# Starts of the SBUF buffers in a two-layer hybrid attention encoder: from multiples of 128 bytes to multiples of 512

## The chip, the cores and the metric

The kernel runs on one core of a Trainium2 chip. The metric is the device time of one execution in microseconds (us); of several executions the median is given. The engines are called PE (TensorE, its weight loads shown apart as PEld), DVE (VectorE), ACT (ScalarE), POOL (GpSimd) and SP (SyncE, which issues most of the DMAs).

## The reference, cut to what matters

Two layers over a sequence of 512 tokens of width 1024, all in float32. Each layer normalises its input, projects it with one wide matrix, runs three attention branches side by side, and merges them through sigmoid gates.

```python
for l in range(DEPTH):                                  # DEPTH = 2
    mod = c_act @ w_ada[l] + b_ada[l]
    shift, scale, gate = [m[:, None, :] for m in split_cols(mod, (D, D, D))]
    h = rms_norm(x, g_pre[l]) * (1.0 + scale) + shift
    (cq, ckv, kr, za, qb_, kb_, vb_, zb, qc, kc, vc, zc, gcols) = split_cols(h @ w_in[l], IN_SPLITS)
    o_a = (mla_branch(cq, ckv, kr, ...) * jax.nn.silu(za)) @ w_o_mla[l]
    o_b = (swa_branch(qb_, kb_, vb_, sink[l], swa_bias) * jax.nn.silu(zb)) @ w_o_swa[l]
    o_c = (diff_branch(qc, kc, vc, ...) * jax.nn.silu(zc)) @ w_o_diff[l]
    g = jax.nn.sigmoid(gcols).reshape(B, S, N_BRANCH, D)
    y = (g[:, :, 0] * o_a + g[:, :, 1] * o_b + g[:, :, 2] * o_c) @ w_out[l]
    x = x + gate * rms_norm(y, g_post[l])
```

The branches are multi-head latent attention (MLA, 8 heads), sliding-window attention with sinks (SWA, 8 heads over 2 key heads), and differential attention (4 heads of two score maps each).

## The kernel before, in words

Precision comes from splitting: a float32 operand is written as a high part in the type float32r and a low part that holds the rest, and a product of two split operands is three matmuls, high by high, high by low and low by high (mm3, lines 87 to 90). The normed and transposed input of a layer lies in hTh and hTl for the whole layer. wunit (lines 103 to 117) loads 512 KB of weights into a tile wr, from which ACT writes the high part (wh, line 82) and DVE the low part (wl, line 85); proj_T (lines 464 to 470) then runs 8 x 3 matmuls of 128x128 by 512 columns, with a piece of wh or wl as the stationary operand and a piece of hTh or hTl as the moving one. In pe.matmul(o, a, b) the first input, a, is the stationary operand and b the moving one; the profile names the moving one first (ps_dn<-hTh,wh).

- merge_steps (lines 528 to 571) multiplies the outputs of a branch, split into pairs of tiles u, by the branch's output weights: moving u, stationary wh or wl.
- prep, within mla_attention, makes a head's queries and keys from latents (cl, in tiles big) with weights in the tile x5: moving big, stationary x5.
- The scores take both operands from tiles op; the products with the values take the transposed probabilities (pt) as the moving operand and the values (tiles big) as the stationary one. Transposes on PE (line 704) have ident as the moving operand.
- out_phase (lines 1017 to 1066) multiplies by w_out in two halves of 512 columns, 8 x 4 x 3 matmuls each. Here the weights move, and the stationary operands are the merged tiles in op and pt. In the second half the first two of four weight tiles lie in tiles big (wunit with big true, lines 105 and 106), the other two in wh and wl, so that for each of four row tiles twelve matmuls read big and the next twelve wh and wl.
- At the start, layer0_input (lines 338 to 371) computes three of the gate inputs with weights split into tiles pt: moving hTh or hTl, stationary pt.

The order of the instructions on each engine is set when the program is built, by a scheduler of the framework that goes by a simulated timeline; priorities are given in the code. Tiles are taken by T (lines 64 to 67). A tag has a fixed number of buffers (line 62), and the buffers of a tag get their place, in each partition, when the tag is first used, one after another. A buffer takes its bytes per partition rounded up to 32. The first tile of the program, ident, begins at byte 16,512, which is 128 past a multiple of 512. ident, ones and onesr take 512 bytes each, then mhalf 96 and epsc 32, so that the eight buffers big begin at 18,176, 256 past a multiple of 512; the rest follows in this way. Some small tiles are 32 columns wide although fewer are used (LINE, line 23, in lines 151, 168, 177 and 398), which makes 128 bytes of each and keeps every large buffer on a multiple of 128. Where the buffers begin, in bytes past a multiple of 512, the same for all buffers of a tag, since their sizes are multiples of 512:

| buffers | before |
|---|---|
| ident, ones, onesr, rq, rk | 128 |
| big, hTh, hTl, o, op, wr, p, u, pt, zz | 256 |
| wh, wl, tf, ta, x5, kp | 384 |

Within a tile the matmuls read from offsets that are multiples of 512 bytes, so these numbers hold for their operands too (the matmuls of one column, and two that read the small tile rb, apart).

Of the kernel before, what the change touches and what calls it, by code (L numbers as in the profile page):

```python
# [17 lines left out]
P = 128  # L18
S = 512
D = 1024  # L20
KT = D // P
NT = S // P
LINE = 32
DEPTH = 2
EPS = 1e-6
NEG = -1e30
# [25 lines left out]
def hybrid_kernel(ctx, tc, x, c, w_ada, b_ada, g_pre, g_post, w_in, g_q, w_uq, g_kv, w_ukv,  # L52
# [6 lines left out]
    pe, act, dve, pool, sp = nc.tensor, nc.scalar, nc.vector, nc.gpsimd, nc.sync  # L59
# [4 lines left out]
    def T(tag, shape, dt=F32, bufs=None):  # L64
        count[0] += 1
        return sb.tile(shape, dt, tag=tag, name=f"{tag}_{count[0]}",
                       bufs=bufs or BUFS.get(tag, 1))

    def stat(n):
        return T("st", [P, n], F32, 24)  # L70
# [3 lines left out]
    def Q(tag):  # L74
        count[0] += 1
        return ps.tile([P, S], F32, tag=tag, name=f"ps_{tag}_{count[0]}", bufs=PB[tag])
# [41 lines left out]

    WOFF = [100]

    ident = T("ident", [P, P])
    make_identity(nc, ident)
    ones = T("ones", [P, P])
    dve.memset(ones, 1.0)
    onesr = T("onesr", [P, P], F32R)
    dve.tensor_copy(out=onesr, in_=ones)
    mhalf = T("mhalf", [P, 24])
    dve.memset(mhalf, -0.5)
    epsc = T("epsc", [P, 1])
    dve.memset(epsc, EPS)  # L130

    x1d = dr.tile([S, D], F32, tag="x1d", name="x1d")
# [15 lines left out]
        return res  # L148

    xt0 = [T("big", [P, D]) for _ in range(NT)]  # L150
    cT = T("cT", [P, LINE])[:, 0:KT]
    sp.dma_start(out=cT, in_=c.rearrange("b (p k) -> p (b k)", k=KT))
    src0 = mod_load(0, 0, 1, ("wh", "wl"))
    prm = [T("tf", [P, P]) for _ in range(2)]
# [2 lines left out]
    for k, src, n in ((PR_GQ, g_q, 2), (PR_GKV, g_kv, 1), (PR_GSUB, g_sub, 1)):  # L157
        pool.dma_start(out=prm[1][k - 32:k - 32 + n * DEPTH, :],
                       in_=src.rearrange("l (a b) -> (l a) b", b=P))
# [3 lines left out]
    prT = []  # L163

    for i, n in enumerate((32, PR_ROWS - 32)):
        prps = Q("tr")
        pe.transpose(prps[:, 0:n], prm[i][0:n, :], ident[0:n, 0:n])
        prT.append(T(f"prT{i}", [P, LINE])[:, 0:n])
        dve.tensor_copy(out=prT[i], in_=prps[:, 0:n])

    def par(l, k, i=0, n=1):
        lo = k + l * PR_STEP[k] + i
        return prT[lo // 32][:, lo % 32:lo % 32 + n]

    th = stat(KT)
    act.activation(out=th, in_=cT, func=AF.Tanh, scale=0.5)
    cact = T("cact", [P, LINE])[:, 0:KT]
    dve.scalar_tensor_tensor(out=cact, in0=th, scalar=1.0, in1=cT, op0=ALU.add, op1=ALU.mult)
    dve.tensor_scalar(out=cact, in0=cact, scalar1=0.5, scalar2=None, op0=ALU.mult)

    amul = [T(f"amul{l}", [P, KT]) for l in range(DEPTH)]
    ashf = [T(f"ashf{l}", [P, KT]) for l in range(DEPTH)]

    stts, amuls, sums = [], [], []

# [209 lines left out]

    rq = T("rq", [P, S])
    rk = T("rk", [P, NT, 64])
    sinkt = T("sinkt", [P, LINE])[:, 0:DEPTH * 8]
    lam_neg = []
    gsub = []  # L400
    bias_s = []
# [2 lines left out]
    def setup_small():  # L404
        sp.dma_start(out=rk, in_=rope_k.rearrange("(t p) c -> p t c", p=P))
        sp.dma_start(out=rq, in_=rope_q)
        sp.dma_start(out=sinkt, in_=sink.rearrange("(o l) h -> o (l h)", o=1).broadcast_to([P, DEPTH * 8]))
        for l in range(DEPTH):
            li = 0.8 - 0.6 * math.exp(-0.3 * l)
            lt = T("tf", [P, 4, 64])  # L410
            for i, src in enumerate((lam_q1, lam_k1, lam_q2, lam_k2)):
                sp.dma_start(out=lt[:, i], in_=src[l:l + 1, :].broadcast_to([P, 64]))
            e = stat(2)
            for i in range(2):
                dve.tensor_tensor(out=lt[:, 2 * i], in0=lt[:, 2 * i], in1=lt[:, 2 * i + 1],
                                  op=ALU.mult)
                dve.tensor_reduce(out=e[:, i:i + 1], in_=lt[:, 2 * i], axis=AX.X, op=ALU.add)
            act.activation(out=e, in_=e, func=AF.Exp)
            nl = T(f"nl{l}", [P, 1])
            dve.tensor_scalar(out=nl, in0=e[:, 1:2], scalar1=e[:, 0:1], scalar2=-li,  # L420
                              op0=ALU.subtract, op1=ALU.add)
            lam_neg.append(nl)
            gs = T(f"gs{l}", [P, 1])
            dve.tensor_scalar(out=gs, in0=par(l, PR_GSUB), scalar1=0.5 * (1.0 - li), scalar2=None,
                              op0=ALU.mult)
            gsub.append(gs)
# [721 lines left out]
    with behind(loads[-1]):  # L1148
        setup_small()
# [70 lines left out]
```

## Time and profile before

| what | value |
|---|---|
| median of 3 runs | 1195.54 us (1195.54 to 1196.23) |
| the profiled execution | 1194.84 us |
| its span, first to last instruction | 1192.9 us |
| mean granted TensorE clock | 0.992 |
| matmul records | 5428 |
| DMA | 146.86 MB, 123 GB/s on the mean |

A row of the timeline gives the start and the length of an instruction, its engine and line, what it writes and reads, and the shapes. The length of a matmul is modelled to the end of its way through the array, while the next one starts before that; so the distance between starts is read from the first numbers of two rows, and the length from the second. In a row of groups stand the count, the busy time, the mean length in ns and the idle time before it. A row of windows gives, for a stretch of the span, its length, the busy time and the instructions of PE, PEld, DVE, ACT and POOL, the granted clock, the share of the DMA engines and GB/s.

### The profile page before, as it was taken

The page shows a single profiled execution, that of the slowest core. Times are in us where ns is not written, and L with a number is a line of the kernel's source. Part 1 is how long each engine was busy: PE and PEld are TensorE (multiplying, and loading weights), DVE is VectorE, ACT ScalarE, POOL GpSimd, SP SyncE. Part 2 cuts the span into 40 slices and gives each one's busy share as a digit, 9 for nine tenths or more (in the row PEclk, how much of TensorE's full clock was granted, in tenths as well). Part 3 has the DMA queues.
Part 4 walks back from the last instruction along what each step waited for, and adds up shares of the span by engine and source line. Part 5 has one row for each costly group of instructions (what it writes and reads, how often), then busy time and mean ns, then how long its engine had stood idle before and what let it go on. Part 6 is the DMA issues. An engine that isn't in the chain of part 4 may idle for free.

```text
span 1192.9 us, 15536 instructions
## 1 busy us (share of the span) xinstructions
PE 1163.9 (98%) x5428; PEld 949.2 (80%) x5428; DVE 845.5 (71%) x1754; ACT 632.3 (53%) x1250; POOL 182.5 (15%) x226
## 2 busy tenths in 40 slices
PE   5899999999999999999999999999999999999997
PEld 4778788878887888888888888888888888888886
DVE  7956676998865687866577557688785468776554
ACT  5454464655543457654357446565555345665432
POOL 4310212111210010102111011122121001010120
PEclk8899999999999999999999999999999999999999
DMA  9637532255355333443454433224433433334442
GB/s 328 200 89 215 179 110 71 75 157 168 104 155 159 98 85 81 114 118 112 149 176 136 109 104 87 72 67 121 140 102 84 107 85 90 87 101 111 133 161 86
DMA packets 169522, 146.86 MB, mean 123 GB/s; under 512 B 7679, under 2 KB 146999, under 8 KB 169444
## 3 DMA queue, kind: packets, MB, share of 16 engines
q1 hardware_dynamic: 166148, 140.08, 40.8%
q10 hardware_dynamic: 3168, 5.77, 1.4%
q8 instruction: 43, 0.70, 0.2%
q14 instruction: 35, 0.29, 0.1%
q0 software_dynamic: 128, 0.01, 0.0%
HBM read 135.83 MB, written 14.20 MB: 126 GB/s over the span
## 4 chain that ended last, share of the span: by engine, by line
PE 85%; DVE 6%; DMA 4%; issue 3%; POOL 1%; ACT 1%; SPq 1%; DVEq 0%; POOLq 0%; ACTq 0%
PE ps_dn L88 20%; PE ps_dn L90 20%; PE ps_dn L89 20%; PE ps_tr L704 5%; PE ps_sc L90 2%; PE ps_sc L88 2%; PE ps_sc L89 2%; PE ps_av L713 1%; PE ps_av L714 1%; DMA wr<-in_w_ada 1%; PE ps_sc L953 1%; PE ps_sc L952 1%; DVE o L205 1%; DMA wr<-in_w_in 1%; PE ps_pj L88 1%
## 5 line engine op out<-in xcount | busy, mean ns | idle before, releaser
L88 PE MATMUL ps_dn<-hTh,wh 128*128 128x512 f32 x840 | 335.8, 400 | 0.4 <-DVE zz L479 0.3
L90 PE MATMUL ps_dn<-hTh,wl 128*128 128x512 f32 x840 | 334.2, 398 | 0.3 <-DVE wl L85 0.3
L89 PE MATMUL ps_dn<-hTl,wh 128*128 128x512 f32 x840 | 333.9, 398 | 0.0
L85 DVE TENSOR_TENSOR wl<-wr,wh 128x1024 fp32r<-128x1024 f32 x141 | 178.9, 1269 | 105.2 <-ACT wh L82 104.3
L82 ACT ACTIVATE wh<-wr 128x1024 fp32r<-128x1024 f32 x141 | 149.1, 1058 | 174.2 <-PE ps_dn L89 119.0
L90 PEld LDWEIGHTS ps_dn<-hTh,wl 128*128 128x128 f32 x840 | 158.3, 188 | 36.5 <-DVE wl L85 0.7
L88 PEld LDWEIGHTS ps_dn<-hTh,wh 128*128 128x128 f32 x840 | 158.6, 189 | 35.5 <-DVE zz L479 0.6
L89 PEld LDWEIGHTS ps_dn<-hTl,wh 128*128 128x128 f32 x840 | 158.6, 189 | 35.1
L82 ACT ACTIVATE pt<-ps_tr 128x512 fp32r<-128x512 f32 x136 | 79.0, 596 | 69.0 <-PE ps_tr L704 67.8
L85 DVE TENSOR_TENSOR pt<-ps_tr,pt 128x512 fp32r<-128x512 f32 x136 | 92.3, 686 | 32.3 <-ACT pt L82 31.4
L775 POOL TENSOR_SCALAR p<-p,st 128x512 f32<-128x512 f32 x64 | 52.2, 835 | 283.9 <-DVE st L773 246.8
L704 PE MATMUL ps_tr<-ident,p 128*128 128x128 f32 x544 | 92.3, 273 | 0.5 <-POOL p L775 0.3
L704 PEld LDWEIGHTS ps_tr<-ident,p 128*128 128x128 f32 x544 | 69.6, 141 | 19.7 <-POOL p L775 1.2
L90 PE MATMUL ps_dn<-u,wl 128*128 128x512 f32 x192 | 76.6, 399 | 0.0
L88 PE MATMUL ps_dn<-u,wh 128*128 128x512 f32 x192 | 76.6, 399 | 0.0
L89 PE MATMUL ps_dn<-u,wh 128*128 128x512 f32 x192 | 76.0, 396 | 0.0
L963 POOL TENSOR_SCALAR ta<-ta,st 128x512 f32<-128x512 f32 x32 | 26.8, 837 | 312.6 <-DVE st L962 132.0
L894 POOL TENSOR_SCALAR p<-p,st 128x256 f32<-128x256 f32 (+1 forms) x64 | 41.4, 666 | 160.2 <-DVE st L892 126.2
L770 DVE TENSOR_REDUCE st<-ps_sc 128x1 f32<-128x512 f32 x64 | 43.5, 687 | 22.0 <-PE ps_sc L90 21.5
L771 ACT ACTIVATE p<-ps_sc,st 128x512 f32<-128x512 f32 x64 | 43.8, 686 | 28.0 <-DVE st L770 27.5
L886 ACT ACTIVATE p<-p,st 128x256 f32<-128x256 f32 (+1 forms) x64 | 35.6, 557 | 20.6 <-DVE st L884 20.4
L959 ACT ACTIVATE p<-p,st 128x512 f32<-128x512 f32 x32 | 23.1, 723 | 38.1 <-DVE st L957 38.0
(345 smaller groups left out, 2109.6 us busy)
## 6 DMA issues: line engine op xcount, KB each, us to landing
wr<-in_w_in SPq DMA_DIRECT2D x105, 512.0 KB, 3.8
wr<-in_w_ada SPq DMA_DIRECT2D x32, 512.0 KB, 3.6
wr<-in_w_out SPq DMA_DIRECT2D x16, 512.0 KB, 3.7
big<-in_w_ada SPq DMA_DIRECT2D x10, 512.0 KB, 7.8
big<-in_x SPq DMA_DIRECT2D x8, 512.0 KB, 5.3
wr<-in_w_o_mla SPq DMA_DIRECT2D x8, 512.0 KB, 3.5
wr<-in_w_o_swa SPq DMA_DIRECT2D x8, 512.0 KB, 3.5
wr<-in_w_o_diff SPq DMA_DIRECT2D x8, 512.0 KB, 3.6
```

The costliest lines, as they stand in the source:

```text
L82: return act.activation(out=out_, in_=in_, func=AF.Copy, scale=scale)
L85: return (eng or dve).tensor_tensor(out=out_, in0=a, in1=b, op=ALU.subtract)
L88: pe.matmul(o, ah, bh, start=start, stop=False)
L89: pe.matmul(o, ah, bl, start=False, stop=False)
L90: pe.matmul(o, al, bh, start=False, stop=stop)
L704: pe.transpose(tr[:, i * P:(i + 1) * P], b, ident)
L770: dve.tensor_reduce(out=nm[:, t:t + 1], in_=s, axis=AX.X, op=ALU.max, negate=True)
L771: act.activation(out=pr[:, t], in_=s, func=AF.Exp, bias=nm[:, t:t + 1], accum_out=sm[:, t:t + 1])
L775: pool.tensor_scalar(out=pr[:, t], in0=pr[:, t], scalar1=rr[:, t:t + 1], scalar2=1.0, op0=ALU.mult, op1=ALU.mult)
L886: act.activation(out=pr[:, i, :w], in_=pr[:, i, :w], func=AF.Exp, bias=nm[:, i:i + 1], accum_out=sm[:, i:i + 1])
L894: pool.tensor_scalar(out=pr[:, i, :w], in0=pr[:, i, :w], scalar1=rr[:, i:i + 1], scalar2=1.0, op0=ALU.mult, op1=ALU.mult)
L963: pool.tensor_scalar(out=pc[1], in0=pc[1], scalar1=rr[:, 1:2], scalar2=1.0, op0=ALU.mult, op1=ALU.mult)
```

## The change

The small tiles that live through the whole program are taken first, before ident: mhalf (now 8 columns), epsc, cT, cact, amul and ashf for both layers, lamc (new, 4 columns, which takes the place of nl0, nl1, gs0 and gs1) and sinkt (24 columns). Together they take 384 bytes, so that ident begins at 16,896, a multiple of 512. LINE is gone.

```diff
-LINE = 32
...
+    mhalf = T("mhalf", [P, 8])
+    epsc = T("epsc", [P, 1])
+    cT = T("cT", [P, KT])
+    cact = T("cact", [P, KT])
+    amul = [T(f"amul{l}", [P, KT]) for l in range(DEPTH)]
+    ashf = [T(f"ashf{l}", [P, KT]) for l in range(DEPTH)]
+    lamc = T("lamc", [P, 2 * DEPTH])
+    sinkt = T("sinkt", [P, 24])
     ident = T("ident", [P, P])
...
-    mhalf = T("mhalf", [P, 24])
     dve.memset(mhalf, -0.5)
-    epsc = T("epsc", [P, 1])
     dve.memset(epsc, EPS)
...
-    cT = T("cT", [P, LINE])[:, 0:KT]
...
-        prT.append(T(f"prT{i}", [P, LINE])[:, 0:n])
+        prT.append(T(f"prT{i}", [P, 32])[:, 0:n])
...
-    cact = T("cact", [P, LINE])[:, 0:KT]
...
-    amul = [T(f"amul{l}", [P, KT]) for l in range(DEPTH)]
-    ashf = [T(f"ashf{l}", [P, KT]) for l in range(DEPTH)]
...
-    sinkt = T("sinkt", [P, LINE])[:, 0:DEPTH * 8]
...
-            nl = T(f"nl{l}", [P, 1])
+            nl = lamc[:, 2 * l:2 * l + 1]
...
-            gs = T(f"gs{l}", [P, 1])
+            gs = lamc[:, 2 * l + 1:2 * l + 2]
```

As built, every buffer of 512 bytes or more a partition that TensorE reads (ident, ones, onesr, big, hTh, hTl, op, wh, wl, u, p, pt, tf, ta, x5), and wr, o, zz, rq, rk and kp besides, begins at a multiple of 512 bytes. The instructions of every engine stand in the same order in both programs, with the same waits, and nothing else in them differs but the addresses, the width of the memset of mhalf, and the names lamc for nl and gs.

More of the change, by code (lines that the diff above doesn't have):

```diff
@@ L406, in setup_small @@
         sp.dma_start(out=rq, in_=rope_q)
-        sp.dma_start(out=sinkt, in_=sink.rearrange("(o l) h -> o (l h)", o=1).broadcast_to([P, DEPTH * 8]))
+        sp.dma_start(out=sinkt[:, 0:DEPTH * 8], in_=sink.rearrange("(o l) h -> o (l h)", o=1).broadcast_to([P, DEPTH * 8]))
         for l in range(DEPTH):
```

## The prediction

> **What bounds the kernel now.** I read the page first, then the windows, then TensorE's timeline. The page gives the span and the busy times, and the chain that ended last.
>
> ```profile
> span 1192.9 us, 15536 instructions
> PE 1163.9 (98%) x5428; PEld 949.2 (80%) x5428; DVE 845.5 (71%) x1754; ACT 632.3 (53%) x1250; POOL 182.5 (15%) x226
> PE 85%; DVE 6%; DMA 4%; issue 3%; POOL 1%; ACT 1%; SPq 1%; DVEq 0%; POOLq 0%; ACTq 0%
> ```
>
> PE is busy 98% of the span and 85% of the last chain runs on it; DVE, the next engine, is at 71%. The windows say where PE is the whole story:
>
> ```profile
> 0.00:60.00 60.00, 40.39 (x187) 35.60 (x188) 48.84 (x122) 28.48 (x55) 24.77 (x29) 0.89 0.79 262
> 60.00:130.00 70.00, 69.11 (x304) 54.37 (x303) 44.48 (x115) 35.95 (x94) 4.81 (x6) 1.00 0.57 162
> 130.00:260.00 130.00, 127.68 (x618) 102.38 (x617) 101.65 (x173) 75.70 (x156) 26.94 (x33) 0.99 0.38 110
> 260.00:600.00 340.00, 339.92 (x1580) 277.10 (x1579) 245.37 (x521) 178.81 (x323) 44.66 (x56) 1.00 0.43 123
> 640.00:1165.00 525.00, 525.00 (x2448) 426.71 (x2447) 363.83 (x740) 284.07 (x552) 73.95 (x91) 1.00 0.37 106
> ```
>
> The first engine column is PE. From 130 us on it idles for 2.3 us in the first window and 0.1 us in the 865 us of the last two. So the time after 130 us is the number of matmuls times the distance from one start to the next, which I call a slot. A matmul's 0.39 us reaches into the next slot, so a wait shorter than some 0.16 us does not show as idle time. Only two things can shorten this program without taking matmuls away: shorter slots, or fewer such hidden waits.
>
> **What the change does to each engine.** Every engine's instructions stand in the same order in both programs, with the same waits; only addresses differ, and one memset (128x24 becomes 128x8). So the question is what a start address does to a slot. The trace of before answers a part of it, because its buffers do not all begin alike: big, hTh, hTl, op, u, p, pt and wr begin 256 bytes past a multiple of 512, and wh, wl, tf, ta and x5 begin 384 past one. In the last phase (out_phase, second half) the same loop takes its moving operand for twelve matmuls from big, then for twelve from wh and wl, with the stationary operands in op and pt (256) throughout. The timeline of PE, the first matmul of each twelve, and two from inside the twelves of big:
>
> ```profile
> 1164.51 0.39 PE L88 MATMUL ps_dn<-big,op 128*128 128x512 f32 x1
> ...
> 1165.89 0.39 PE L88 MATMUL ps_dn<-big,op 128*128 128x512 f32 x1
> ...
> 1167.25 0.40 PE L88 MATMUL ps_dn<-wh,op 128*128 128x512 f32 x1
> ...
> 1170.04 0.39 PE L88 MATMUL ps_dn<-big,op 128*128 128x512 f32 x1
> ...
> 1172.78 0.40 PE L88 MATMUL ps_dn<-wh,op 128*128 128x512 f32 x1
> ...
> 1175.57 0.39 PE L88 MATMUL ps_dn<-big,op 128*128 128x512 f32 x1
> ...
> 1178.31 0.40 PE L88 MATMUL ps_dn<-wh,op 128*128 128x512 f32 x1
> ...
> 1181.10 0.39 PE L88 MATMUL ps_dn<-big,op 128*128 128x512 f32 x1
> ...
> 1183.83 0.40 PE L88 MATMUL ps_dn<-wh,op 128*128 128x512 f32 x1
> ```
>
> Twelve slots with big take 2.74, 2.74, 2.74 and 2.73 us: 228.1 ns each. Twelve with wh and wl take 2.79 three times: 232.5 ns. That is 4.4 ns for the same shapes in the same loop, and the two sorts alternate, so it is no drift of the clock. Inside a twelve of big the first slots after the switch are the longer ones: from 1165.89 to 1167.25 six slots take 1.36 us, 226.7 ns. The other operand behaves alike: with the moving operand at 256 all the time, the stationary one at 384 (wh, wl) or at 256 (big, pt):
>
> ```profile
> 70.67 0.39 PE L88 MATMUL ps_dn<-hTh,pt 128*128 128x512 f32 x1
> ...
> 72.71 0.49 PE L630 MATMUL ps_tr<-ident,ta 128*128 128x128 f32 x3
> 1097.61 0.39 PE L88 MATMUL ps_dn<-u,wh 128*128 128x512 f32 x1
> ...
> 1100.39 0.39 PE L88 MATMUL ps_av<-pt,big 128*128 128x512 f32 x1
> ...
> 1101.75 0.40 PE L88 MATMUL ps_dn<-hTh,wh 128*128 128x512 f32 x1
> 1140.33 0.40 PE L90 MATMUL ps_dn<-u,wl 128*128 128x512 f32 x1
> 1140.57 0.40 PE L88 MATMUL ps_dn<-u,wh 128*128 128x512 f32 x1
> 1140.81 0.40 PE L89 MATMUL ps_dn<-u,wh 128*128 128x512 f32 x1
> ```
>
> Nine slots hT by pt take 2.04 us and six slots pt by big take 1.36 us: 226.7 ns both times, with both operands at 256. Twelve slots u by wh between them take 2.78 us, 231.7 ns. So in three places, in three kinds of loop, a pair with one operand at 384 costs 232.3 ns (11.15 us over the 48 slots of the four twelves) and a pair with both at 256 between 226.7 (an undisturbed run) and 228.1 (a run of twelve after a switch). After the change all of them begin at 0, which no row of before shows. I take 0 to be as good as 256: the step seen lies between starts that are and are not multiples of 256, and 0 is one. The saving of a mixed slot is then 4.2 to 5.6 ns; I take 4.9, the middle, since inside attention transposes and waits will go on disturbing the runs.
>
> **How many slots.** The groups of PE between 130 us and the end:
>
> ```profile
> L88 PE MATMUL ps_dn<-hTh,wh 128*128 128x512 f32 x781 | 312.2, 400 | 0.1
> L88 PE MATMUL ps_dn<-u,wh 128*128 128x512 f32 x192 | 76.6, 399 | 0.0
> L714 PE MATMUL ps_av<-pt,big 128*64 128x512 f32 x72 | 29.4, 409 | 0.0
> L704 PE MATMUL ps_tr<-ident,p 128*128 128x128 f32 x544 | 92.3, 273 | 0.5 <-POOL p L775 0.3
> L88 PE MATMUL ps_pj<-big,x 128*128 128x512 f32 x34 | 13.5, 397 | 0.0
> L88 PE MATMUL ps_dn<-wh,op 128*128 128x512 f32 x32 | 12.7, 397 | 0.0
> L88 PE MATMUL ps_dn<-big,op 128*128 128x512 f32 x32 | 12.5, 390 | 0.0
> L823 PE MATMUL ps_pj<-ident,tf 128*128 128x128 f32 x40 | 6.3, 272 | 0.0
> ```
>
> Each mm3 issues L88, L89 and L90, so the projections are 3 x 781 = 2343, the merges 3 x 192 = 576 and prep's x5 weights 3 x 34 = 102. out_phase has 2 halves x 8 x 4 x 3 = 192 a layer, 384 in both, of which 3 x 32 = 96 read big and 288 read wh and wl. Mixed slots: 2343 + 576 + 102 + 288 = 3309. Saving: 3309 x 4.9 ns = 16.2 us. Nearly all matmuls of 512 columns that are left (some 700: scores from op, values from big) have both operands at 256, but many follow a mixed one; they gain from 0 to 4.2 ns each, 0 to 3.0 us, and I take 1.5. Transposes are charged nothing: with the other operand in p (256) or tf (384) they take 273 and 272 ns.
>
> What passes to the end: with 0.1 us idle in 865, nearly all. Part comes back as waits where DVE, ACT and PE hand each other tiles in attention; between none and a fifth, I take a twentieth. So 17.7 x 0.95 = 16.8 us. If DVE were closer to its limit than 71%, it would be late next.
>
> **Edits costed at nothing.** The memset is smaller by 16 columns at the start of DVE's queue; lamc holds what nl and gs held, written by the same instructions. Transfers: wh (384) and big (256) take 512 KB of the same tensor, in the same stretch, equally long, so I price the destination's start at zero, also in the first 60 us, where DMA is the busy one. DVE with inputs at 256 and 256 (o, zz) and at 256 and 384 (big, tf) differs by 1 ns, so I charge the other engines nothing.
>
> ```profile
> big<-in_w_ada SPq DMA_DIRECT2D x10, 512.0 KB, 7.8
> wh<-in_w_ada SPq DMA_DIRECT2D x3, 512.0 KB, 7.8
> L570 DVE TENSOR_TENSOR big<-big,tf 128x512 f32<-128x512 f32 x16 | 11.0, 687 | 0.0
> L796 DVE SCALAR_TENSOR_TENSOR o<-o,zz 128x512 f32<-128x512 f32 x16 | 10.8, 686 | 0.1
> ```
>
> **The rivals.**
> *Nothing to gain.* The 4.4 ns belongs to something that goes along with wh, wl and x5 and not to their start: place in memory, or being written anew for each use. Against it: pt, stationary at 70.67, is written anew in each step of its loop as wh is, and has the short slot, and wh as moving operand is as long as wh as stationary one. The time would be the 1195.5 of now. Chance 0.08. [...]
>
> *Multiples of 512 are better still.* If 384 to 256 saves a step of 5.6 and 256 to 0 saves another, slots go to 221.1: 3309 x 11.2 + 700 x 5.6 = 41.0 us, less a twentieth 38.9, time 1156.6. For it: within one group the slots still scatter, 228.1 on the mean of twelve and 226.7 at the end of it, so something is left to settle. Against it: the step seen is one between multiples and non-multiples of 256, and no row tells 0 from 256. Chance 0.06. [...]
>
> *Slower: all streams begin alike.* Where all buffers start at the same place in 512 bytes, moving and stationary reads and the other engines' streams may meet at the same place. The price: slots of 240 ns, as the two from 1140.33 to 1140.81, in place of 232.3, would cost 3309 x 7.7 = 25.5 us, time 1221.0; it decides from a mean slot above 232.3. Against it: operands both at 256 begin alike too, and have the shortest slots. Chance 0.04.
>
> **How the numbers follow.** The profiled execution took 1194.84 us, 1.9 more than its span, and 0.7 less than the median of the three timed runs; the sum is a difference, so I take it from the median: 1195.54 - 16.8 = 1178.7. The forecast's chance is 0.82. Its own bounds: 3309 x 4.2 = 13.9 less a fifth is 11.1 us (1184.4), and 3309 x 5.6 + 3.0 = 21.5 us (1174.0). The range reaches on to 1164 for a part of a second step and to 1189 for half an effect. A difference under 0.2% (2.4 us) cannot be told from none. Faster 0.88, same 0.08, slower 0.04.
>
> **What would show it.** Right: the twelves of wh and of big in the last phase equally long, 2.72 to 2.74 us; the mean of L88 hTh,wh down from 400 to about 391, as big,op has it; PE still busy to 0.1 us in the long windows. If slots shorten but the span does not, PE would show waits on DVE or ACT in attention. Wrong: slots of 232 with both operands at 0 (the start is not the cause), slots under 225 (0 is better than 256), or a gain outside the mixed groups, in the first 60 us or in the transposes.

## The result and the profile after

The changed kernel takes 1180.25 us (1178.78 to 1180.60, 4 runs) beside 1195.54 us (1193.59 to 1196.23) of the kernel before in the same session: a ratio of 0.9872, interval 0.9855 to 0.9889, so 15.3 us less. Its profiled execution took 1178.78 us, 16.06 less than that of before (1194.84). In its profile mm3's three matmuls are L87, L88 and L89 (L88 to L90 before).

The page, with the span, the busy times and the chain that ended last:

```profile
span 1176.7 us, 15536 instructions
PE 1146.0 (97%) x5428; PEld 946.0 (80%) x5428; DVE 844.2 (72%) x1754; ACT 631.5 (54%) x1250; POOL 181.3 (15%) x226
PE 84%; DVE 6%; DMA 3%; issue 3%; ACT 1%; POOL 1%; SPq 0%; DVEq 0%; POOLq 0%; ACTq 0%
```

The instructions are as many as before on every engine. PE's busy time fell by 17.9 us (from 1163.9), DVE's by 1.3 and ACT's by 0.8; the chain still runs on PE. The windows, PE first:

```profile
130.00:260.00 130.00, 127.14 (x625) 102.78 (x624) 102.85 (x174) 75.25 (x156) 27.85 (x36) 0.99 0.38 110
260.00:600.00 340.00, 339.36 (x1599) 280.84 (x1598) 247.82 (x524) 180.55 (x328) 44.41 (x53) 1.00 0.44 126
640.00:1165.00 525.00, 525.00 (x2487) 433.22 (x2486) 366.44 (x735) 281.86 (x542) 72.72 (x90) 1.00 0.37 105
```

In the 525 us from 640 on, PE is busy throughout in both kernels, and gets through 2487 matmuls where it got through 2448. The granted clock reads 1.00 in both. A fully busy engine that does 1.6% more in the same time at the same clock is what a shorter slot looks like: the busy time of such a window cannot show it, the count behind the busy time does.

The same place of out_phase as in the prediction, the first matmul of each twelve:

```profile
1148.74 0.39 PE L87 MATMUL ps_dn<-big,op 128*128 128x512 f32 x1
...
1151.46 0.39 PE L87 MATMUL ps_dn<-wh,op 128*128 128x512 f32 x1
...
1154.18 0.39 PE L87 MATMUL ps_dn<-big,op 128*128 128x512 f32 x1
...
1156.90 0.39 PE L87 MATMUL ps_dn<-wh,op 128*128 128x512 f32 x1
```

Every twelve takes 2.72 us now, 226.7 ns a slot, from big as from wh and wl: the 2.79 of the one are gone, and so is the part of the 2.74 of the other that the switch had cost. The groups of PE and the loads, as the prediction listed them:

```profile
L87 PE MATMUL ps_dn<-hTh,wh 128*128 128x512 f32 x780 | 308.1, 395 | 0.6 <-DVE op L807 0.6
L87 PE MATMUL ps_dn<-u,wh 128*128 128x512 f32 x192 | 75.9, 395 | 0.0
L87 PE MATMUL ps_dn<-wh,op 128*128 128x512 f32 x32 | 12.5, 392 | 0.0
L87 PE MATMUL ps_dn<-big,op 128*128 128x512 f32 x32 | 12.5, 390 | 0.0
L704 PE MATMUL ps_tr<-ident,p 128*128 128x128 f32 x544 | 92.4, 273 | 0.9 <-POOL p L775 0.6
L823 PE MATMUL ps_pj<-ident,tf 128*128 128x128 f32 x40 | 6.3, 272 | 0.0
big<-in_w_ada SPq DMA_DIRECT2D x10, 512.0 KB, 7.6
wh<-in_w_ada SPq DMA_DIRECT2D x3, 512.0 KB, 7.4
```

Where one operand had been at 384, the mean length fell by 4 or 5 ns (400 to 395, 399 to 395, 397 to 392); big,op stayed at 390, the transposes at 273 and 272, and the transfers moved by 0.2 and 0.4 us. Where in the program the time came from shows in the first and last starts of two groups, of before:

```profile
L88 PE MATMUL ps_dn<-u,wh x192: 387/392/481, 293.1 to 1144.1; 128*128 128x512 f32 x192
L704 PE MATMUL ps_tr<-ident,p x544: 270/272/421, 132.7 to 1096.6; 128*128 128x128 f32 x182
```

and of after:

```profile
L87 PE MATMUL ps_dn<-u,wh x192: 387/389/481, 291.0 to 1128.8; 128*128 128x512 f32 x192
L704 PE MATMUL ps_tr<-ident,p x544: 270/272/421, 131.3 to 1082.4; 128*128 128x128 f32 x182
```

The new kernel is ahead by 1.4 us at its first transpose, by 2.1 at its first merge, by 14.2 at its last transpose and by 15.3 at its last merge. So the gain grows with the matmuls, and no single place makes it.

To compare kernels more sharply than by lengths, I took the distance from start to start of every projection and merge of 512 columns whose neighbours on both sides are projections or merges too, from all rows of PE's timeline up to 250 ns. There are some 2,500 of them in each trace. Their mean is 232.5 ns before and 227.7 after. I call this the clean slot.

### The profile page after: what moved, and what is told of

Same layout as the page of the kernel before. It is cut to its first block, busy times and chain, and to the rows that moved or that the text cites. A ratio compares the mean times of both kernels' runs of the same rounds, so it can differ in the third digit from the quotient of the medians.

```text
span 1176.7 us, 15536 instructions
## 1 busy us (share of the span) xinstructions
PE 1146.0 (97%) x5428; PEld 946.0 (80%) x5428; DVE 844.2 (72%) x1754; ACT 631.5 (54%) x1250; POOL 181.3 (15%) x226
## 4 chain that ended last, share of the span: by engine, by line
PE 84%; DVE 6%; DMA 3%; issue 3%; ACT 1%; POOL 1%; SPq 0%; DVEq 0%; POOLq 0%; ACTq 0%
PE ps_dn L87 20%; PE ps_dn L89 20%; PE ps_dn L88 19%; PE ps_tr L704 5%; PE ps_sc L89 2%; PE ps_sc L87 2%; PE ps_sc L88 2%; PE ps_av L714 1%; PE ps_av L713 1%; PE ps_sc L952 1%; PE ps_sc L953 1%; DMA wr<-in_w_in 1%; DVE o L206 1%; PE ps_pj L87 1%; PE ps_pj L88 1%
## 5 line engine op out<-in xcount | busy, mean ns | idle before, releaser
L87 PE MATMUL ps_dn<-hTh,wh 128*128 128x512 f32 x840 | 331.8, 395 | 1.4 <-DVE zz L479 0.8
L89 PE MATMUL ps_dn<-hTh,wl 128*128 128x512 f32 x840 | 330.5, 393 | 0.4 <-DVE wl L84 0.4
L88 PE MATMUL ps_dn<-hTl,wh 128*128 128x512 f32 x840 | 330.1, 393 | 0.0
L87 PEld LDWEIGHTS ps_dn<-hTh,wh 128*128 128x128 f32 x840 | 158.2, 188 | 33.2 <-PE ps_dn L89 1.0
L89 PEld LDWEIGHTS ps_dn<-hTh,wl 128*128 128x128 f32 x840 | 158.0, 188 | 33.3 <-DVE wl L84 0.9
L88 PEld LDWEIGHTS ps_dn<-hTl,wh 128*128 128x128 f32 x840 | 158.1, 188 | 31.7
L87 PE MATMUL ps_dn<-u,wh 128*128 128x512 f32 x192 | 75.9, 395 | 0.0
L89 PE MATMUL ps_dn<-u,wl 128*128 128x512 f32 x192 | 75.9, 395 | 0.0
L88 PE MATMUL ps_dn<-u,wh 128*128 128x512 f32 x192 | 75.2, 391 | 0.0
```

Source lines behind the costliest of these rows:

```text
L87: pe.matmul(o, ah, bh, start=start, stop=False)
L88: pe.matmul(o, ah, bl, start=False, stop=False)
L89: pe.matmul(o, al, bh, start=False, stop=stop)
```

## The experiments

All kernels but one are the changed kernel with its instructions in the same order and up to 512 bytes of padding a partition between tiles; the one (two widths) is the kernel before with two tiles widened. Nothing is left out of the computation. Each was timed in three rounds beside the kernel before, whose median was 1193.2 to 1195.0 us in these sessions. Ratios are to it.

| operands begin at (mod 256) | median us | ratio (interval) | clean slot, ns |
|---|---|---|---|
| all at 128 | 1179.22 | 0.9872 (0.9857 to 0.9887) | 227.7 |
| all at 256 (mod 512) | 1178.14 | 0.9862 (0.9845 to 0.9878) | 227.7 |
| all at 32 | 1181.41 | 0.9883 (0.9866 to 0.9899) | 227.7 |
| wh, wl at 256 (mod 512), rest 0 | 1178.72 | 0.9866 (0.9851 to 0.9880) | 227.7 |
| wh, wl at 128, rest 0 | 1194.59 | 0.9998 (0.9988 to 1.0007) | 232.5 |
| wh, wl at 64, rest 0 | 1195.72 | 1.0017 (1.0007 to 1.0026) | 233.3 |
| wh, wl at 32, rest 0 | 1194.63 | 1.0008 (0.9998 to 1.0017) | 233.1 |
| wh, wl at 224, rest 0 | 1194.94 | 1.0001 (0.9991 to 1.0010) | 233.2 |
| wh, wl at 192, rest 0 | 1185.93 | 0.9937 (0.9922 to 0.9951) | 229.6 |
| wl alone at 128 | 1188.71 | 0.9954 (0.9939 to 0.9969) | 231.4 |
| hTl alone at 128 | 1185.76 | 0.9941 (0.9924 to 0.9958) | 230.3 |
| kernel before, two tiles wider | 1179.54 | 0.9865 (0.9850 to 0.9880) | 227.8 |

**Own start, or the distance between the two operands?** The kernel before has operands at 256 and 384 only. There a pair that is "mixed" has one operand off the multiples of 256, as the prediction put it, and also has its two operands 128 bytes apart; the two readings cannot be told apart. They part when everything is moved together. All at 128:

```diff
+    T("pad", [P, 32])
     ident = T("ident", [P, P])
```

> The changed kernel with 128 bytes of padding ahead of ident: every large buffer begins 128 past a multiple of 512, moving and stationary operands alike. Theory A (each operand's own start counts, and a start that is no multiple of 256 lengthens a slot): every slot of 512 columns is at least as long as the mixed ones of the kernel before, 232.3 ns, so about 1196 to 1197 us; if two such operands cost twice, 237 ns and about 1217 us. Theory B (what counts is that both operands begin alike within 512 bytes, wherever that is): slots stay at 227.7 ns and the time at 1180 us.

The window of 525 us and the first matmuls of the twelves:

```profile
640.00:1165.00 525.00, 525.00 (x2487) 433.28 (x2486) 367.51 (x735) 282.78 (x544) 72.72 (x90) 1.00 0.37 105
```

```profile
1149.27 0.39 PE L87 MATMUL ps_dn<-big,op 128*128 128x512 f32 x1
...
1151.99 0.39 PE L87 MATMUL ps_dn<-wh,op 128*128 128x512 f32 x1
...
1154.71 0.39 PE L87 MATMUL ps_dn<-big,op 128*128 128x512 f32 x1
```

2487 matmuls and twelves of 2.72 us, as after: with no operand on a multiple of 256, the whole gain is there. That refutes the reading on which the prediction rested, and speaks for the distance. All at 256 (the same line with 64 columns):

> The changed kernel with 256 bytes of padding ahead of ident: every large buffer begins 256 past a multiple of 512. Theories A (starts modulo 256) and B (both alike) expect 1180 us and slots of 227.7 ns, no difference from the changed kernel. Theory C (a multiple of 512 is better than one of 256) expects longer slots: 1 ns more would be 4 us, 1184 us.

It took 1178.14 us, with a clean slot of 227.7. A start at 0 is no better than one at 256, so the rival of a second step is refuted. All at 32 (8 columns), run later, when it was known how small a distance costs:

> The changed kernel with 32 bytes of padding ahead of ident: every large buffer begins 32 past a multiple of 512, moving and stationary operands alike. If only the difference between the two operands counts, 1179 us and slots of 227.7 ns, as with 128 and 256 of padding. If a start that is no multiple of 128 costs by itself, slots of 233 ns as in w32 and about 1195 us.

1181.41 us and a clean slot of 227.7: with all operands at 32, 128 or 256 the slot is that of 0, so their own start made no difference in these four runs.

**One side alone.** Now only wh and wl move, by a pad before them, and a second pad puts the tiles behind them back:

```diff
+    T("pada", [P, 32])
     src0 = mod_load(0, 0, 1, ("wh", "wl"))
+    T("padb", [P, 96])
```

> The changed kernel with padding around wh and wl alone, so that these six buffers begin 128 past a multiple of 512 and all others at 0. Their slots are 2343 + 576 + 288 of the 3309 mixed ones. Theories A and B both expect these 3207 slots at 232.3 in place of 227.7 ns: 14.8 us more than 1180, so about 1195 us, nearly all of what the change gained. If the gain came from elsewhere (x5, ident, transfers, other engines), the time stays near 1180 us.

```profile
640.00:1165.00 525.00, 525.00 (x2447) 426.50 (x2446) 366.23 (x745) 286.15 (x559) 72.61 (x91) 1.00 0.37 105
```

```profile
1163.07 0.39 PE L87 MATMUL ps_dn<-big,op 128*128 128x512 f32 x1
...
1165.82 0.40 PE L87 MATMUL ps_dn<-wh,op 128*128 128x512 f32 x1
...
1168.61 0.39 PE L87 MATMUL ps_dn<-big,op 128*128 128x512 f32 x1
```

This is the kernel before again: 2447 matmuls (2448), twelves of 2.75 and 2.79 us, 1194.59 us. So the places of these two tags, and no other edit of the change, carry its effect. It does not refute "multiples of 256" by itself, since wh and wl are at 128 here; with the run of all at 128 it does. wh and wl at 256 (pads of 64 and 64 columns), which asks whether the distance counts by 256 or by 512 bytes:

> The changed kernel with padding around wh and wl alone, so that these six buffers begin 256 past a multiple of 512 and all others at 0: the two operands of 3207 slots begin apart, but each at a multiple of 256. Theory A (starts modulo 256) expects 1180 us and 227.7 ns; theory B (both alike within 512 bytes) expects 232.3 ns and about 1195 us; theory C (512 better than 256) something between.

```profile
640.00:1165.00 525.00, 525.00 (x2486) 433.26 (x2486) 366.02 (x734) 281.14 (x540) 72.92 (x90) 1.00 0.36 105
```

1178.72 us and a clean slot of 227.7: a distance of 256 costs nothing here, and the multiples of 512 that the change aims at are more than this kernel needs.

**How does the cost depend on the distance?** wh and wl at 64, 32, 192 and 224 (pads of 16 and 112, 8 and 120, 48 and 80, 56 and 72 columns):

> The changed kernel with wh and wl alone beginning 64 past a multiple of 512, all others at 0. By the runs so far a difference of 128 between the two operands costs 4.7 ns a slot in 3207 slots, and a difference of 256 costs nothing. Theory D1 (the two starts must lie in the same half of 256 bytes) expects no cost: 1179 us, slots 227.7 ns. Theory D2 (the cost grows with the difference, up to 128) expects half: 2.4 ns a slot, 7.5 us more, about 1187 us. Theory D3 (some difference is better than none) expects shorter slots, under 226 ns, and less than 1176 us.

> The changed kernel with wh and wl alone beginning 32 past a multiple of 512, all others at 0. Theory D1 (same half of 256 bytes) expects no cost: 1179 us. Theory D2 (cost grows with the difference) expects a quarter: 1.2 ns a slot, 3.7 us, about 1183 us. Theory D3 (some difference is better than none) expects under 1176 us here or at 64 or 192.

> The changed kernel with wh and wl alone beginning 192 past a multiple of 512, all others at 0. Theory D1 (same half of 256 bytes) expects the full cost, 4.7 ns a slot and about 1194 us, since 192 lies in the other half than 0. Theory D2 (cost grows with the difference modulo 256, here 64 short of 256) expects half, about 1187 us, as for 64. Theory D3 expects it may be below 1176 us.

> The changed kernel with wh and wl alone beginning 224 past a multiple of 512, all others at 0. The run with 192 cost 2 ns a slot in the projections (stationary operand at 192, moving at 0) and 6 ns in out_phase (the other way round), those with 32 and 64 cost 5 to 6 ns in both. Theory F1 (every difference that is no multiple of 256 costs about the same, and 192 was a lucky phase) expects 233 ns and about 1194 us. Theory F2 (the cost depends on the direction: little when the stationary operand begins a little below the moving one, modulo 256) expects under 229.6 ns in the projections, 232 or more in out_phase, and 1180 to 1185 us.

The 525 us of the four, in this order:

```profile
640.00:1165.00 525.00, 525.00 (x2443) 425.71 (x2442) 363.99 (x741) 284.20 (x550) 72.74 (x91) 1.00 0.35 105
```

```profile
640.00:1165.00 525.00, 525.00 (x2445) 425.55 (x2444) 364.16 (x740) 284.27 (x552) 72.88 (x91) 1.00 0.35 105
```

```profile
640.00:1165.00 525.00, 525.00 (x2468) 429.92 (x2467) 366.36 (x736) 283.25 (x544) 73.22 (x90) 1.00 0.35 105
```

```profile
640.00:1165.00 525.00, 525.00 (x2446) 425.36 (x2445) 364.43 (x741) 284.23 (x552) 72.63 (x91) 1.00 0.37 105
```

64, 32 and 224 cost the whole step and a little more, 5.4 to 5.6 ns a slot against 4.8 for 128. None of the sizes written down for 64 and 32 was right: the cost does not shrink with the distance (5.6 at 64, 5.4 at 32). The run of 224 came out as the theory had it that all distances but multiples of 256 (and, in part, 192) cost the same.

192 is the exception, and only one way round. In the projections wh and wl are stationary; in out_phase they move, and the stationary operands (op, pt) begin at 0. There 192 costs the whole step, and 64 behaves as 192 does in the projections. A twelve of wh and wl, and the start of the next twelve, of the run with 192:

```profile
1163.29 0.39 PE L87 MATMUL ps_dn<-wh,op 128*128 128x512 f32 x1
...
1166.09 0.39 PE L87 MATMUL ps_dn<-big,op 128*128 128x512 f32 x1
```

and of the run with 64:

```profile
1172.54 0.40 PE L87 MATMUL ps_dn<-wh,op 128*128 128x512 f32 x1
...
1175.30 0.40 PE L87 MATMUL ps_dn<-big,op 128*128 128x512 f32 x1
```

These take 2.80 us (233.3 ns a slot) and 2.76 (230). Counted from the moving operand to the stationary one, modulo 256, the distance in out_phase is 64 where wh and wl are at 192, and 192 where they are at 64. So the exception goes with a stationary operand 192 past the moving one. It is not always short: just before these twelves, the run with 64 holds 233.3 ns over 85 slots in a row. Nor does out_phase gain by it, since the twelves of big beside these take 2.77 us with 64 and 2.74 with 192.

The trace of 192 shows two patterns in the projections and merges. In its clean stretches of eight slots and more, 70 of 98 have a mean of 229 ns, 18 of 230, and 10 of 233. Two stretches of the same kind of matmul, u by wh or wl, every third one, first:

```profile
360.01 0.39 PE L87 MATMUL ps_dn<-u,wh 128*128 128x512 f32 x1
...
360.70 0.39 PE L87 MATMUL ps_dn<-u,wh 128*128 128x512 f32 x1
...
361.39 0.39 PE L87 MATMUL ps_dn<-u,wh 128*128 128x512 f32 x1
...
1130.28 0.40 PE L87 MATMUL ps_dn<-u,wh 128*128 128x512 f32 x1
...
1130.98 0.40 PE L87 MATMUL ps_dn<-u,wh 128*128 128x512 f32 x1
...
1131.68 0.40 PE L87 MATMUL ps_dn<-u,wh 128*128 128x512 f32 x1
```

Three slots take 0.69 us in one stretch and 0.70 in the other; from the unrounded starts 229.0 and 233.3 ns a slot, with the same operands at the same distance. Within a stretch the slots repeat: 226, 229, 232 over and over in the one, 233, 233, 234 in the other. A fixed charge for an address would give one number. Where the distance is 64 there is but one: of the 98 clean stretches of the run with 64, none has a mean under 232.6. What sets a stretch of the run with 192 on one of the patterns, no row shows.

**One operand of the three.** A product of two split operands is three matmuls: L87 reads hTh and wh, L88 hTl and wh, L89 hTh and wl. With wl alone at 128, only L89 has its operands apart:

```diff
+            if len(loads) == 1:
+                T("pada", [P, 32])
...
     src0 = mod_load(0, 0, 1, ("wh", "wl"))
+    T("padb", [P, 96])
```

> The changed kernel with wl alone beginning 128 past a multiple of 512; wh and all others at 0. In a projection the three matmuls of mm3 run hTh by wh, hTl by wh, hTh by wl. Theory E1 (a matmul's moving operand and its own stationary one must agree) expects the slot of hTh by wl alone to lengthen to some 232 ns. Theory E2 (the moving operand of a matmul and the stationary one that is loaded meanwhile for the next must agree) expects the slot of hTl by wh alone to lengthen. Either lengthens one slot of three, 1069 x 4.7 = 5.0 us, about 1184 us; if the cost spreads to the neighbours, up to 1189 us.

The groups of PE from 130 us on:

```profile
L87 PE MATMUL ps_dn<-hTh,wh 128*128 128x512 f32 x781 | 308.6, 395 | 0.1
L88 PE MATMUL ps_dn<-hTl,wh 128*128 128x512 f32 x781 | 310.7, 398 | 0.0
L89 PE MATMUL ps_dn<-hTh,wl 128*128 128x512 f32 x781 | 311.7, 399 | 0.0
```

and of after, of which the first is listed further up (395):

```profile
L88 PE MATMUL ps_dn<-hTl,wh 128*128 128x512 f32 x781 | 307.1, 393 | 0.0
L89 PE MATMUL ps_dn<-hTh,wl 128*128 128x512 f32 x781 | 307.3, 394 | 0.0
```

So the matmul that uses wl is longer by 5, and so is the one before it, L88, whose own operands are both at 0; the one behind it is unchanged. The clean slots of the projections say the same: 228.3, 232.3 and 233.4 ns. While L88 streams hTl, the stationary operand of L89, wl, is being loaded (its load starts 3 ns after L88, by the median of 768 such pairs in the trace of after), which would fit for L88; why L89's own slot is long too, I can't tell. Each theory had half of this. Next hTl alone at 128, the moving operand of L88, with wh and wl at 0:

```diff
-        return T("hTh", [P, KT, S], F32R), T("hTl", [P, KT, S], F32R)
+        hh = T("hTh", [P, KT, S], F32R)
+        first = not amuls
+        if first:
+            T("pada", [P, 32])
+        hl = T("hTl", [P, KT, S], F32R)
+        if first:
+            T("padb", [P, 96])
+        return hh, hl
```

> The changed kernel with hTl alone beginning 128 past a multiple of 512, all others at 0: the counterpart of wl128, with the moving operand shifted in place of the stationary one. It touches one matmul of three in the projections, hTl by wh. With wl shifted, two groups lengthened: the matmul that uses wl and the one before it, during which wl is loaded. Theory G1 (a stationary operand is read over two slots, its load and the one after, a moving operand in its own slot alone) expects the group of hTl by wh alone to lengthen, by 5 ns in the mean, and 781 to 840 slots x 5 = 4 us: about 1183 us. Theory G2 (whatever is shifted, the neighbours suffer) expects two groups longer, as in wl128, and 1187 us.

```profile
L87 PE MATMUL ps_dn<-hTh,wh 128*128 128x512 f32 x781 | 310.3, 397 | 0.2 <-DVE op L814 0.2
L88 PE MATMUL ps_dn<-hTl,wh 128*128 128x512 f32 x781 | 310.3, 397 | 0.0
L89 PE MATMUL ps_dn<-hTh,wl 128*128 128x512 f32 x781 | 308.3, 395 | 0.0
```

The moving operand does it as the stationary one does: its own matmul is longer by 4, the one before by 2, the one behind by 1; the clean slots are 232.8, 230.4 and 228.8. The merges (u by wh and wl), which don't read hTl, stay at 227.8 and 228.1. The time, 1185.76 us, lies between the two figures expected. The effect is of the pair and of its neighbours in time, and how it divides among them is open.

**The smallest change.** If only distances count, the kernel before needs two widths and none of the new order of tiles:

```diff
-    cT = T("cT", [P, LINE])[:, 0:KT]
+    cT = T("cT", [P, 2 * LINE])[:, 0:KT]
...
-    sinkt = T("sinkt", [P, LINE])[:, 0:DEPTH * 8]
+    sinkt = T("sinkt", [P, 2 * LINE])[:, 0:DEPTH * 8]
```

This puts wh, wl, tf, hTh, hTl, op, u, p and pt at 0 and big at 256, and leaves ident, ones, onesr, x5 and ta at 128.

> The kernel before with two numbers changed: cT and sinkt are taken 64 columns wide in place of 32. ident, ones, onesr stay at 128 and big at 256, but wh, wl, tf, hTh, hTl, op, u, p and pt come to 0, so that all differences are multiples of 256 except those of x5 (102 slots) and of the transposes. If the difference of the operands is the whole cause, this gives what the change gives but for 102 x 4.7 ns = 0.5 us: about 1180 us. If the order of the small tiles, lamc, or multiples of 512 have a part, it stays above: up to 1194 us.

```profile
640.00:1165.00 525.00, 525.00 (x2483) 432.72 (x2482) 366.54 (x735) 281.80 (x542) 72.57 (x90) 1.00 0.36 105
```

```profile
L88 PE MATMUL ps_pj<-big,x 128*128 128x512 f32 x33 | 13.2, 401 | 0.0
L704 PE MATMUL ps_tr<-ident,p 128*128 128x128 f32 x544 | 92.4, 274 | 0.8 <-POOL p L775 0.5 <-DVE pt L85 0.2
```

1179.54 us, alike with the whole change. Two pairs of 512 columns are still 128 apart, big by x5 (big,x) and pt by onesr. Both keep long slots: 231.0 ns clean for the first (401 in the row; after has 227.7), and 233.4 over the 20 of the second that take up to 250 ns (after has 228.2). Transposes with ident 128 bytes from p take 274 ns against 273: for 128 columns no effect is seen in the length.

None of these versions beats the changed kernel by more than the runs scatter: 1178.14, 1178.72, 1179.22, 1179.54 and 1180.25 us are alike.

## Why the prediction was right, and where its reason was not

**The number.** 1178.7 was forecast, 1180.25 measured; -16.8 us against -15.3 by the medians and -16.1 by the profiled executions.

**The saving of a mixed slot** held: 4.9 ns was taken, the clean slots give 232.5 - 227.7 = 4.8. That w128 returns the whole gain shows that this is the cause.

**The reason for it failed.** The step of the prediction that reads "I take 0 to be as good as 256: the step seen lies between starts that are and are not multiples of 256" had the right consequence and the wrong rule. Starts at 128 (1179.22 us) and at 32 (1181.41 us) are as good, if both operands have them. What counts in these runs is the distance between the two starts: 227.7 ns a slot at 0 and at 256 bytes (mod 512), 229.6 to 233.3 at 32, 64, 128, 192 and 224. Had the change moved everything by 128, the same reasoning would have forecast no gain, and the run of all at 128 has the whole of it. So the number owes something to luck: this change brings all large operands to one start, and there both readings say the same. The prediction's evidence against "all streams begin alike" (both at 256 have the shortest slots) was the right observation: it was this rival, with its sign turned, that came nearest to what the runs show.

**The number of slots** was too small. 3309 was counted in groups from 130 us on, but there are projections earlier: of all 840 projections of L88 in the page of before (below), 781 lie behind 130 us. With these 3 x 59 and 18 more slots of prep (3 x 6, since x5 is read 40 times for each line and 34 were counted) the count is 3504; 24 slots of wh by big and 24 of pt by onesr, also with 128 bytes between their operands, make it 3552. The matmuls stand in the same order in both traces, so each slot of before can be set beside its own of after. 3402 of these take no more than 250 ns in both, and together they became shorter by 16.5 us, 4.8 ns each, where the sum had 16.2. Part of the 1.4 us that the new kernel is ahead at its first transpose is from there.

```profile
L88 PE MATMUL ps_dn<-hTh,wh 128*128 128x512 f32 x840 | 335.8, 400 | 0.4 <-DVE zz L479 0.3
```

**Slots that only follow mixed ones** were taken at 1.5 us for some 700, 2.1 ns each. Set side by side in the same way, the scores from op became shorter by 0.60 us (2.1 ns each), pt by big by 0.32 (1.2) and big by op by 0.14 (1.4): 1.1 us.

**What is given back** was taken at a twentieth, 0.9 us, and was about twice that. The page has it: the span less PE's busy time is 29.0 us before (1192.9 - 1163.9) and 30.7 after (1176.7 - 1146.0), 1.7 us more. Most of it is behind 130 us: PE's idle time from 130 to 260 us went from 2.32 to 2.86 us, from 260 to 600 from 0.08 to 0.64, and from 600 to 640 from 0.01 to 0.37. The waits of PE from 130 to 600 us name most of what came there, first of before:

```profile
PE ps_tr L704 <- POOL p L775: 0.3, 1, 0.3
```

and of after:

```profile
PE ps_dn L87 <- DVE op L807: 0.6, 1, 0.6
PE ps_tr L704 <- POOL p L775: 0.6, 2, 0.3
```

A faster PE meets DVE once and POOL twice in the first layer's attention, for 0.9 us more than before. "PE still busy to 0.1 us" thus failed by half a us in one window, in the direction that the prediction had named. 16.5 + 1.1 - 1.7 is 15.9 us; the profiled executions differ by 16.06 and their spans by 16.2. The forecast's 16.8 is near it in part because its terms miss in different directions: the slots by 0.3 us too little, those that follow by 0.4 too much, what is given back by 0.8 too little.

**The mean of L88 hTh,wh** was to fall from 400 to about 391 and fell to 395, while the twelves of out_phase came out as forecast. 391 was near the 390 of big,op, which runs undisturbed. Where projections run undisturbed they have it: between 908 and 956 us the mean of after is 391 (55 matmuls), between 260 and 600, in the first layer's attention, 394. Before has 396 and 399 there, so what lengthens them in attention stayed. The difference (5) was the thing to forecast, not the level.

**Costed at nothing, and rightly:** the transposes (273 and 272 before and after), DVE, the memset. The loads landed 0.2 and 0.4 us sooner (7.6 and 7.4 against 7.8); this was not followed up, since w128, which has wh elsewhere, gives back the whole time.

**The rivals.** "Nothing to gain" fell with the result. "Multiples of 512 are better still" fell with all at 256 and with wh and wl at 256. "All streams begin alike" fell with every run at one common start.

## What to carry to other kernels

Where TensorE is busy throughout with matmuls of 512 columns of float32r, try the buffers of its two operands at starts that are alike or 256 bytes apart (mod 512): that took 227.7 ns a slot here, against 232.5 to 233.3 at 32, 64, 128 and 224 and 229.6 at 192. Where they begin did not matter here (all at 0, 32, 128 and 256 took 227.7 each), and two small tiles made wider did it (1179.54 us). Look for such costs by the distance between starts and by the number of instructions in a fully busy window, and by a loop that reads two buffers in turn: a busy share shows nothing (in the 525 us from 640 on, PE is busy for 525.00 before and after). And where the traces hold only two values of an address, no rule about the address is known yet: move everything together, and then one side alone, before believing one.

## What the runs showed of the hardware

- A matmul of 128x128 by 512 columns in float32r, in a stretch of its kind, takes 227.7 ns from start to start where its operands begin 0 or 256 bytes apart (mod 512), and 232.5 to 233.3 ns where the stationary tile (wh or wl) begins 32, 64, 128 or 224 past the moving one. At 192 the means of 98 stretches are 229 ns (70 of them), 230 (18) and 233 (10). With wh and wl moving instead, in out_phase, a twelve takes 233.3 ns a slot with them at 192 and 230 with them at 64 (a run of 85 there 233.3).
- A kernel's time moved by 1.2% (1180.25 to 1194.59 us) with nothing changed but the place of wh and wl, and so the distance between two operands of TensorE itself; what in the chip makes the distance count, no run here shows.
- The weight loads don't lengthen with it: PEld's busy time over its count, in the 525 us from 640 on, is 174.3 ns after (433.22 us by 2486) and 174.4 with wh and wl at 128 (426.50 by 2446). The delay shows in the matmuls, in their distance and in their modelled length.
- The shortest mean of twelve slots in a row (each of 200 to 250 ns) is 226.6 ns in the trace of after (2.72 us, from 94.04 us on) and 227.4 in that of before (2.73 us, from 600.75 us on).

Open: why the matmul beside the shifted one is slowed, why a stationary operand 192 past the moving one has two patterns and one 64 past it has one, what distances between those run (96 and 160, say) cost, and whether other element types and fewer columns behave alike.
